# Interleaved rotary embedding: result tiles beside the tiles of x, in place of results written over x

## The chip, the cores and the metric

One core of one Trainium2 chip. The metric is device time in microseconds (us) of one execution. Profiles are of single executions; their span is about 1.8 us shorter than the device time. In the profile's lines DVE is VectorE, ACT is ScalarE, POOL is GpSimd and SP is SyncE; a q after the name (POOLq) is the engine's sequencer, and L56 is line 56 of that run's kernel. A transfer lands when its completion is signalled to the engines that wait for it.

## The reference

```python
# x: (8, 2048, 16, 64) fp32; cos, sin: (2048, 32) fp32
x1, x2 = x[..., 0::2], x[..., 1::2]          # pairs along the head dimension
out1 = x1 * cos - x2 * sin                   # cos, sin per position, the same for all heads
out2 = x1 * sin + x2 * cos
out  = interleave(out1, out2)                # (8, 2048, 16, 64) fp32
```

x and out are 67.1 MB each. There are 8 batches, so one batch is 8.39 MB in fp32, or 4.19 MB once it is cast to bf16.

## The kernel before

A batch is one bf16 tile of 128 partitions x 16 positions x 1024 columns (32 KB per partition). A load reads fp32 from HBM and casts it to bf16 on the way; a store casts back. All big transfers are issued from GpSimd, on one queue. Five tiles hold x, and the rotation is done over x, so the same tile is loaded, rotated, stored, and loaded again. KP is the number of positions in one piece of VectorE's work, NX the number of tiles for x; HEAD and TAIL are the few positions at the start and the end that take another path:

```python
    KP = 4; NX = 5; HEAD = 2; TAIL = 4
    # ... s_tab holds (sin, -sin) pairs, c_tab (cos, cos) pairs, both bf16 ...
    def load(b, k0=0):     # x of batch b from HBM to a tile, cast to bf16
        nc.gpsimd.dma_start(out=tiles[b][:, k0:], in_=x_t[b, :, k0:])
    def store(b, k1=K):
        nc.gpsimd.dma_start(out=out_t[b, :, :k1], in_=tiles[b][:, :k1])
    def rotate(b, k0, k1):
        # ...
        nc.vector.tensor_tensor(out=rows(qt[:, :nk]), in0=rows(xp), in1=tab(s_tab), op=mult)
        nc.vector.tensor_tensor(out=rows(xp), in0=rows(xp), in1=tab(c_tab), op=mult)
        # q_swap: qt with the two members of each pair exchanged
        nc.vector.tensor_tensor(out=x3, in0=x3, in1=q_swap, op=add)

    # first two positions of batch 0, sin and cos come through SyncE and ScalarE; then:
        load(0, HEAD)
        for b in range(1, NX):
            load(b)
        # ... tables ...
        for b in range(B):
            # ... rotate the batch in pieces of KP positions ...
            if b < B - 1:
                store(b)
            if b >= 1 and b - 1 + NX < B:
                load(b - 1 + NX)          # its tile is free when store(b - 1) has landed
        store(B - 1, K - TAIL)
        # the last 4 positions of the last batch: cast by ScalarE (after store B-2 has landed), stored by SyncE
```

## Time and profile before

| what | before |
|---|---|
| device time | 317.53 us, median of 3 runs (317.43 to 317.65) |
| profiled span | 315.8 us |
| VectorE busy | 221.8 us (70%), its last instruction ends at 265.6 us |
| DMA, software queue | 97.0% of the span |
| HBM traffic | 67.63 MB read, 67.11 MB written: 427 GB/s over the span |

The first view is the page's table of 40 slices (each digit is a busy share in tenths) and, below it, its table of queues: packets, megabytes, and the share of the 16 DMA engines' time. The software queue (q0 software_dynamic) holds the transfers that GpSimd issues.

```profile
DVE  0009999999999999999999994799708996000000
...
DMA  9999999999999999999999999999999999999997
...
q0 software_dynamic: 2304, 98.04, 97.0%
```

The Trainium skill, "HBM Reference", section "Specifications (TRN2)", has 358 GB/s per core in its table and, in the text below it, about 425 GB/s for a core that streams alone, bounded by its DMA engines; this kernel runs on one core, and its 427 GB/s, loads and stores together, agree with the second.

VectorE has slack at both ends. The DMA engines have none: 9 in every slice but the last.

The second view is the table of waits of the kernel before: who waited for whom, total us, number of times, longest.

```profile
ACT xt L117 <- DMA out_dram<-xt: 286.8, 1, 286.8
POOL out_dram L59 <- DVE xt L80: 153.9, 5, 50.0
POOL xt L56 <- DMA out_dram<-xt: 95.6, 3, 39.7
...
DVE qt L74 <- DMA xt<-in_x_dram: 16.7, 2, 10.8
```

GpSimd waits 95.6 us for stores before it may issue loads 5, 6 and 7, which is the wait that the change takes away. But a wait of the engine that *issues* transfers is lost time only if the queue runs dry meanwhile.

The third view is GpSimd's part of the order of time: start, duration, engine, line, what was issued, and in brackets the idle time before it.

```profile
121.98 0.53 POOL L56 DMA_DIRECT2D xt<-in_x_dram  x1 [39.72 <-DMA out_dram<-xt]
...
141.30 0.53 POOL L56 DMA_DIRECT2D xt<-in_x_dram  x1 [18.27 <-DMA out_dram<-xt]
...
179.95 0.53 POOL L56 DMA_DIRECT2D xt<-in_x_dram  x1 [37.59 <-DMA out_dram<-xt]
```

The load lines (L56) come out the moment a store has landed, so they date the landings: store 0 at 121.98 us, store 1 at 141.30, and store 2, with load 5 in front of it, at 179.95. One transfer takes 19.3 us and two take 38.65, in order of issue. That is 8.39 MB in 19.3 us: 435 GB/s, counted on the fp32 side. At 54 us GpSimd had issued five loads and a store, six transfers or some 116 us of work, so the queue is full and far behind.

The fourth view gives stretches of the span: VectorE's, ScalarE's and GpSimd's busy time (and instructions), the granted clock, the mean share of the DMA engines, and GB/s on the destination side (a load counts only its bf16 bytes, so pure loads read about half of what pure stores do). The view counts each packet whole in the stretch in which it starts, and one packet of these transfers keeps its DMA engine for about 2.4 us (2.43 us for a load, 2.45 us for a store, in this trace's packet records). So shares can exceed 1.00, shares of stretches of 2 to 3 us swing between about 0.5 and 1.2 while the engines are full, and a row of zeros begins up to 2.4 us before the engines are really empty. Where it matters below, the ends of an empty stretch are read from the packet records in the run's trace, which hold the start and the length of every packet.

```profile
0.00:54.00 54.00, 29.72 (x19) 3.18 (x2) 3.00 (x9) 1.00 0.99 223
54.00:122.00 68.00, 67.01 (x30) 0.00 (x0) 1.10 (x3) 1.00 1.02 285
122.00:180.00 58.00, 57.15 (x26) 0.00 (x0) 2.14 (x5) 1.00 1.01 353
180.00:237.60 57.60, 40.44 (x18) 0.00 (x0) 2.07 (x4) 1.00 1.02 300
237.60:295.60 58.00, 27.51 (x12) 0.00 (x0) 0.53 (x1) 1.00 1.00 429
295.60:316.00 20.40, 0.00 (x0) 3.70 (x2) 0.00 (x0) 1.00 0.88 373
```

The DMA share is full in every stretch up to the last transfer. The packet records say it more sharply: from 5 to 305 us an engine was without a packet for 0.05 us on average.

The last view is two groups of VectorE's instructions, same line at two widths: count, busy us, mean ns.

```profile
L74 DVE TENSOR_TENSOR qt<-xt,s_tab 128x4096 bf16<-128x4096 bf16 x31 | 71.1, 2293 | 17.7 <-DMA xt<-in_x_dram 16.7
...
L74 DVE TENSOR_TENSOR qt<-xt,s_tab 128x2048 bf16<-128x2048 bf16 x2 | 2.4, 1222 | 0.0
```

Doubling the columns from 2048 to 4096 adds 1071 ns, 0.523 ns per column. The Trainium skill, "VectorE: DVE Perf Modes", section "The perf-mode tier table", gives 1224 ns for a bf16 `tensor_tensor` of 2048 columns; the trace agrees (1222 to 1226 ns).

### The profile page before, as it was taken

The numbers are of one execution on the slowest core, as the hardware profiler recorded it, in microseconds if no ns is written. First come the engines' busy times: TensorE is split into PE (matmuls) and PEld (weight loads), VectorE is DVE, ScalarE is ACT, GpSimd is POOL, SyncE is SP. The second block draws the span as 40 slices with busy tenths as digits, with TensorE's granted clock in tenths as the row PEclk, the third lists the DMA queues.
The fourth block names the chain that finished last, engine by engine and source line by source line (L and its number), as shares of the span: only waits on it lengthen the run. The fifth ranks groups of instructions, "written<-read, shape, count | busy, mean of one in ns | idle before, by whom it ended". The sixth has DMA issues, their size and how long they took to land.

```text
span 315.8 us, 198 instructions
## 1 busy us (share of the span) xinstructions
DVE 221.8 (70%) x102; ACT 6.9 (2%) x4; POOL 8.8 (3%) x20
## 2 busy tenths in 40 slices
DVE  0009999999999999999999994799708996000000
ACT  2100000000000000000000000000000000000400
POOL 3000000000000001010000100000000000000000
DMA  9999999999999999999999999999999999999997
GB/s 267 211 248 203 199 208 257 199 199 245 220 199 266 398 465 465 398 332 246 220 398 398 390 208 199 448 481 266 199 266 465 398 398 506 423 398 440 427 427 299
DMA packets 3025, 101.72 MB, mean 322 GB/s; under 512 B 336, under 2 KB 336, under 8 KB 848
## 3 DMA queue, kind: packets, MB, share of 16 engines
q0 software_dynamic: 2304, 98.04, 97.0%
q1 hardware_dynamic: 432, 2.88, 2.4%
q10 hardware_dynamic: 288, 0.79, 0.6%
q14 instruction: 1, 0.01, 0.0%
HBM read 67.63 MB, written 67.11 MB: 427 GB/s over the span
## 4 chain that ended last, share of the span: by engine, by line
another core or an unknown queue 91%; DMA 2%; ACTq 1%; ACT 1%; issue 0%
DMA st<-in_x_dram 2%; ACTq L145 1%; ACT xt L93 1%; ACT L93 0%; ACT xt L117 0%; ACTq L117 0%; ACTq L93 0%
## 5 line engine op out<-in xcount | busy, mean ns | idle before, releaser
L74 DVE TENSOR_TENSOR qt<-xt,s_tab 128x4096 bf16<-128x4096 bf16 (+1 forms) x33 | 73.5, 2228 | 17.7 <-DMA xt<-in_x_dram 16.7
L80 DVE TENSOR_TENSOR xt<-xt,qt 128x4096 bf16<-128x4096 bf16 (+1 forms) x33 | 73.5, 2228 | 1.1
L75 DVE TENSOR_TENSOR xt<-xt,c_tab 128x4096 bf16<-128x4096 bf16 (+1 forms) x33 | 73.5, 2228 | 1.1
L95 DVE CAST s_tab<-sin_sb 128x512 bf16<-128x512 f32 x1 | 0.5, 454 | 23.8 <-DMA sin_sb<-in_sin_dram 23.8
L59 POOL DMA_DIRECT2D out_dram<-xt x8 | 4.3, 533 | 153.9 <-DVE xt L80 153.9
L56 POOL DMA_DIRECT2D xt<-in_x_dram x8 | 4.4, 560 | 96.4 <-DMA out_dram<-xt 95.6
L117 ACT COPY xt<-xt 1x1 bf16<-1x1 bf16 x1 | 0.2, 194 | 286.8 <-DMA out_dram<-xt 286.8
L118 ACT CAST st<-xt 128x4096 f32<-128x4096 bf16 x1 | 3.6, 3598 | 0.0
L93 ACT CAST xt<-st 128x2048 bf16<-128x2048 f32 x1 | 1.9, 1897 | 0.0
L93 ACT ACT_TABLE_LOAD x1 | 1.3, 1283 | 5.7 <-DMA st<-in_x_dram 5.7
L97 DVE CAST c_tab<-cos_sb 128x1024 bf16<-128x1024 f32 x1 | 0.7, 684 | 0.0
L96 DVE TENSOR_SCALAR s_tab<-sin_sb 128x512 bf16<-128x512 f32 x1 | 0.4, 444 | 0.0
L134 POOL MEMSET const-float32-0.0<- 128x1 f32 x1 | 0.1, 99 | 0.2 <-issue 0.2
L134 POOL MEMSET const-bfloat16-1.0<- 128x1 bf16 x1 | 0.1, 102 | 0.0
L134 POOL MEMSET const-float32-1.0<- 128x1 f32 x1 | 0.1, 99 | 0.0
L134 POOL MEMSET const-uint8-127<- 128x1 uint8 x1 | 0.1, 99 | 0.0
## 6 DMA issues: line engine op xcount, KB each, us to landing
xt<-in_x_dram POOLq DMA_DIRECT2D x7, 4096.0 KB, 57.6
out_dram<-xt POOLq DMA_DIRECT2D x1, 6144.0 KB, 53.0
xt<-in_x_dram POOLq DMA_DIRECT2D x1, 3584.0 KB, 22.8
out_dram<-st SPq DMA_DIRECT2D x1, 2048.0 KB, 15.5
st<-in_x_dram ACTq DMA_DIRECT2D x1, 512.0 KB, 5.1
st<-in_x_dram SPq DMA_DIRECT2D x1, 512.0 KB, 4.9
sin_sb<-in_sin_dram ACTq DMA_DIRECT2D x1, 256.0 KB, 22.6
cos_sb<-in_cos_dram SPq DMA_DIRECT2D x1, 256.0 KB, 18.6
```

The lines of the kernel that those rows point to most:

```text
L56: nc.gpsimd.dma_start(out=tiles[b][:, k0:], in_=x_t[b, :, k0:])
L59: nc.gpsimd.dma_start(out=out_t[b, :, :k1], in_=tiles[b][:, :k1])
L74: nc.vector.tensor_tensor(out=rows(qt[:, :nk]), in0=rows(xp), in1=tab(s_tab), op=mult)
L75: nc.vector.tensor_tensor(out=rows(xp), in0=rows(xp), in1=tab(c_tab), op=mult)
L80: nc.vector.tensor_tensor(out=x3, in0=x3, in1=q_swap, op=add)
L93: nc.scalar.copy(out=tiles[0][:, :HEAD], in_=head[:, :HEAD])
L95: nc.vector.tensor_copy(out=s2[:, :, 0], in_=sin_sb)
L96: nc.vector.tensor_scalar_mul(s2[:, :, 1], sin_sb, -1.0)
L97: nc.vector.tensor_copy(out=c_tab.rearrange("p k (i j) -> p (k i) j", j=2), in_=cos_sb.to_broadcast([P, K * D2, 2]),)
L118: nc.scalar.copy(out=tail, in_=tiles[B - 1][:, K - TAIL :])
L134: nc = _bacc.Bacc("TRN2", target_bir_lowering=False, num_devices=1)
L145: with _tile.TileContext(nc) as tc:
```

## The change

The intent: a tile of x is read by VectorE only, the result goes to a tile of its own, so a load waits for VectorE and no longer for a store. The multiply by sin is done over x (x is dead after it), which saves the scratch tile. VectorE's pieces grow from 4 to 8 positions. To find room, x has 3 tiles in place of 5, the results 3, and the staging for the first and last positions and for sin and cos borrows tiles of x.

```diff
-    KP = 4
+    KP = 8
-    NX = 5
+    NX = 3
+    NO = 3
 ...
-        nc.vector.tensor_tensor(out=rows(qt[:, :nk]), in0=rows(xp), in1=tab(s_tab), op=mult)
-        nc.vector.tensor_tensor(out=rows(xp), in0=rows(xp), in1=tab(c_tab), op=mult)
+        nc.vector.tensor_tensor(out=rows(op), in0=rows(xp), in1=tab(c_tab), op=mult)
+        nc.vector.tensor_tensor(out=rows(xp), in0=rows(xp), in1=tab(s_tab), op=mult)
 ...
-        nc.vector.tensor_tensor(out=x3, in0=x3, in1=q_swap, op=add)
+        nc.vector.tensor_tensor(out=o3, in0=o3, in1=x_swap, op=add)
 ...
         load(0, HEAD)
-        for b in range(1, NX):
-            load(b)
+        load(1)
 ... (tables)
+        load(2)            # its tile held sin, cos and the first positions
         for b in range(B):
 ...
-            if b < B - 1:
-                store(b)
-            if b >= 1 and b - 1 + NX < B:
-                load(b - 1 + NX)
-        store(B - 1, K - TAIL)
+            if b + NX < B:
+                load(b + NX)
+            store(b, K if b < B - 1 else K - TAIL)
 ... (the tail as before, from a tile of x's pool)
```

More of the change, by code (lines that the diff above doesn't have):

```diff
@@ L42, with fp32_tile @@
     xpool = ctx.enter_context(tc.tile_pool(name="xpool", bufs=NX))
-    qpool = ctx.enter_context(tc.tile_pool(name="qpool", bufs=1))
-    stage = ctx.enter_context(tc.tile_pool(name="stage", bufs=1))
-    cos_sb = consts.tile([P, K * D2], fp32)
-    sin_sb = consts.tile([P, K * D2], fp32)
+    opool = ctx.enter_context(tc.tile_pool(name="opool", bufs=NO))
     c_tab = consts.tile([P, K, D], bf16)
     s_tab = consts.tile([P, K, D], bf16)
-    tiles = {}
+    xs, os = {}, {}
+    def fp32_tile():
+        return xpool.tile([P, K // 2, HD], fp32, name="xt")
     def load(b, k0=0):
-        if b not in tiles:
-            tiles[b] = xpool.tile([P, K, HD], bf16, name="xt")
-        nc.gpsimd.dma_start(out=tiles[b][:, k0:], in_=x_t[b, :, k0:])
+        if b not in xs:
+            xs[b] = xpool.tile([P, K, HD], bf16, name="xt")
+        nc.gpsimd.dma_start(out=xs[b][:, k0:], in_=x_t[b, :, k0:])
     def store(b, k1=K):
-        nc.gpsimd.dma_start(out=out_t[b, :, :k1], in_=tiles[b][:, :k1])
+        nc.gpsimd.dma_start(out=out_t[b, :, :k1], in_=os[b][:, :k1])
     def rotate(b, k0, k1):
         nk = k1 - k0
-        xp = tiles[b][:, k0:k1]
-        qt = qpool.tile([P, KP, HD], bf16, name="qt")
+        xp = xs[b][:, k0:k1]
+        op = os[b][:, k0:k1]
         def rows(a):
@@ L72, in tab @@
             )
-        nc.vector.tensor_tensor(out=rows(qt[:, :nk]), in0=rows(xp), in1=tab(s_tab), op=mult)
-        nc.vector.tensor_tensor(out=rows(xp), in0=rows(xp), in1=tab(c_tab), op=mult)
-        q_swap = dataclasses.replace(
-            qt, offset=qt.offset + 1, ap=[qt.ap[0], [2, nk * HD // 2], [-1, 2]]
-        )
-        x3 = xp.rearrange("p k (a j) -> p (k a) j", j=2)
-        nc.vector.tensor_tensor(out=x3, in0=x3, in1=q_swap, op=add)
+        nc.vector.tensor_tensor(out=rows(op), in0=rows(xp), in1=tab(c_tab), op=mult)
+        nc.vector.tensor_tensor(out=rows(xp), in0=rows(xp), in1=tab(s_tab), op=mult)
+        x_swap = dataclasses.replace(
+            xp, offset=xp.offset + 1, ap=[xp.ap[0], [2, nk * HD // 2], [-1, 2]]
+        )
+        o3 = op.rearrange("p k (a j) -> p (k a) j", j=2)
+        nc.vector.tensor_tensor(out=o3, in0=o3, in1=x_swap, op=add)
     with tc.manual_schedule():
-        head = stage.tile([P, TAIL, HD], fp32, name="st")
+        pre = fp32_tile()
+        cos_sb = pre[:, HEAD, : K * D2]
+        sin_sb = pre[:, HEAD + 1, : K * D2]
         for k in range(HEAD):
             q = (nc.sync, nc.scalar)[k % 2]
-            q.dma_start(out=head[:, k : k + 1], in_=x_t[0, :, k : k + 1])
+            q.dma_start(out=pre[:, k : k + 1], in_=x_t[0, :, k : k + 1])
         nc.sync.dma_start(out=cos_sb, in_=cos_t)
@@ L89 @@
         load(0, HEAD)
-        for b in range(1, NX):
-            load(b)
-        nc.scalar.copy(out=tiles[0][:, :HEAD], in_=head[:, :HEAD])
+        load(1)
+        nc.scalar.copy(out=xs[0][:, :HEAD], in_=pre[:, :HEAD])
         s2 = s_tab.rearrange("p k (i j) -> p (k i) j", j=2)
@@ L100 @@
         )
+        load(2)
         for b in range(B):
-            if b == 0:
-                rotate(b, 0, HEAD)
-                rotate(b, HEAD, KP)
-            for k0 in range(KP if b == 0 else 0, K, KP):
+            os[b] = opool.tile([P, K, HD], bf16, name="ot")
+            for k0 in range(0, K, KP):
                 rotate(b, k0, k0 + KP)
-            if b < B - 1:
-                store(b)
-            if b >= 1 and b - 1 + NX < B:
-                load(b - 1 + NX)
-        store(B - 1, K - TAIL)
-        tail = stage.tile([P, TAIL, HD], fp32, name="st")
-        nc.scalar.copy(out=tiles[B - 2][:1, 0, :1], in_=tiles[B - 1][:1, K - 1, :1])
-        nc.scalar.copy(out=tail, in_=tiles[B - 1][:, K - TAIL :])
-        nc.sync.dma_start(out=out_t[B - 1, :, K - TAIL :], in_=tail)
+            if b + NX < B:
+                load(b + NX)
+            store(b, K if b < B - 1 else K - TAIL)
+        tail = fp32_tile()
+        nc.scalar.copy(out=os[B - 2][:1, 0, :1], in_=os[B - 1][:1, K - 1, :1])
+        nc.scalar.copy(out=tail[:, :TAIL], in_=os[B - 1][:, K - TAIL :])
+        nc.sync.dma_start(out=out_t[B - 1, :, K - TAIL :], in_=tail[:, :TAIL])
 _INS = ['x', 'cos', 'sin']
```

## The prediction

> **What bounds the kernel now.** The 16 DMA engines, from start to end. The slice row for DMA is 9 in 39 of 40 slices; the queue table gives the software queue 97.0% of the span. VectorE is busy 70% and done at 265.6 of 315.8 us (order of time). The waits give landings on that queue: store 0 at 121.98 us, store 1 at 141.30, store 2 at 179.95 (load 5 ahead of it), load 6 at 199.03, load 7 at 237.67 (with store 3), store 6 at 295.6 (with stores 4, 5). That is 19.3 us per 8.39 MB of fp32, load or store, alternating or in a row, in order of issue: 435 GB/s. The Trainium skill, "DMA: Bandwidth & Descriptors", section "Where 436 GB/s comes from", states 435.2 GB/s for the 16 engines; the trace agrees, counted on the fp32 side. 16 transfers of 19.3 us are 309 us; the start (first bytes, sin, cos) adds about 4 us and the end 1 to 2.
>
> **What the change does.**
> - Removes the waits of loads 5 to 7 for stores 0 to 2 (95.6 us of GpSimd waiting). None of it is on the critical path: the queue held issued work throughout.
> - Halves VectorE's instruction count. 2048 columns take 1.22 us, 4096 take 2.293, so 8192 should take 4.43 us (estimate). Six per batch with the 0.035 us step between: 26.8 us against 27.9. VectorE busy falls from 221.8 to about 214 us, off the path.
> - Adds: load 2 waits for the tables (about 25 us; the staging lies in its buffer); the result tile of batch b waits for store b-3.
> - Bytes moved: unchanged.
>
> **Replaying the queue**, 19.3 us each, in issue order L0 L1 L2 L3 S0 L4 S1 L5 S2 L6 S3 L7 S4 S5 S6 S7:
> L2 is issued at 25, queue busy to 43. VectorE ends batch 0 at about 52 and issues L3, S0 (queue busy to 62). Batch 1 ends 79 (queue busy to 100); batch 2, 106 (139); batch 3, 132 (177); batch 4 waits for store 1, ends 165 (216); batch 5, 204 (255); batch 6, 243 (274); batch 7, 281 (293). The queue never runs dry; the thinnest margins are 10 us after batch 0 and 12 us at the end. VectorE's new idle time (about 40 us in batches 4 to 7) costs nothing. The tail is unchanged: ScalarE waits for store 6 at about 295.5 us, casts in 3.6 us, and the last 2 MB share the engines with store 7.
>
> **Predicted time: 317.4 us, range 315.3 to 320.0.** Faster by over 2%: 0.02. Within 2%: 0.95. Slower by over 2%: 0.03.
>
> **Right if:** DMA row 9 in all slices to the end, software queue near 97%. GpSimd's waits name VectorE alone; VectorE now waits for stores before the c_tab multiply, 6 to 12 us in each of batches 4 to 7. VectorE busy near 214 us, 4430 ns each at 8192 columns, ending near 281 us. ScalarE's tail copy released at about 295.5 us.
> **Wrong if:** a slice of DMA clearly below 9 in mid-span (near 52-62 or 281-293 us), ScalarE's copy released later than 298 us, or pairs of load and store taking other than 38.6 us.
>
> **What would make it wrong.** A queue that runs dry because VectorE starts late (sin lands at 23.8 us now; 10 us later would cost) or takes longer per column at 8192. Strict alternation of loads and stores running at another rate than long runs of one kind (unlikely: both show 19.3 us).

## The result, and the profile after

| what | before | after |
|---|---|---|
| device time, median of 6 runs each | 317.48 us (317.40 to 317.65) | 317.51 us (317.35 to 317.71) |
| profiled span | 315.8 us | 315.7 us |
| VectorE busy | 221.8 us | 212.8 us |
| VectorE's last instruction ends | 265.6 us | 283.5 us |

The ratio is 1.0001, with a 95% interval of 0.9989 to 1.0014. Ratios here are the mean time of one kernel's runs over that of the other's of the same rounds, so not quite the ratio of the medians quoted. Executions over 1.5% slower than the fastest of the same kernel are left out of the means.

The same views, after. The slices and the software queue:

```profile
DVE  0009999999999999619992299913999049990000
...
DMA  9999999999999999999999999999999999999996
...
q0 software_dynamic: 2304, 98.04, 97.0%
```

VectorE's row has changed its shape (gaps of idle time from the middle on, and work until later), the DMA row has not, but for one tenth in its last slice.

The waits after. GpSimd waits for VectorE only; what waits for stores now is VectorE, before its first multiply of a batch (and ScalarE at the tail, as before).

```profile
ACT ot L116 <- DMA out_dram<-ot: 286.6, 1, 286.6
POOL xt L57 <- DVE ot L81: 137.4, 5, 35.1
POOL out_dram L60 <- DVE ot L81: 113.8, 3, 38.2
DVE ot L75 <- DMA out_dram<-ot: 45.7, 4, 12.1
```

GpSimd's order of time after (loads are L57). Load 2 goes out when the tables are built; from then on each load and the store beside it are issued as VectorE ends a batch, here load 3 and store 0:

```profile
25.74 0.53 POOL L57 DMA_DIRECT2D xt<-in_x_dram  x1 [23.29 <-DVE c_tab L100]
52.20 0.53 POOL L57 DMA_DIRECT2D xt<-in_x_dram  x1 [25.93 <-DVE ot L81]
52.72 0.54 POOL L60 DMA_DIRECT2D out_dram<-ot  x1
```

VectorE's order of time after: the four multiplies that waited for a result tile, and the last instruction.

```profile
140.95 4.42 DVE L75 TENSOR_TENSOR ot<-xt,c_tab 128x8192 bf16<-128x8192 bf16 x1 [9.53 <-DMA out_dram<-ot]
...
179.53 4.42 DVE L75 TENSOR_TENSOR ot<-xt,c_tab 128x8192 bf16<-128x8192 bf16 x1 [11.98 <-DMA out_dram<-ot]
...
218.23 4.42 DVE L75 TENSOR_TENSOR ot<-xt,c_tab 128x8192 bf16<-128x8192 bf16 x1 [12.10 <-DMA out_dram<-ot]
...
256.88 4.42 DVE L75 TENSOR_TENSOR ot<-xt,c_tab 128x8192 bf16<-128x8192 bf16 x1 [12.05 <-DMA out_dram<-ot]
...
279.05 4.43 DVE L81 TENSOR_TENSOR ot<-ot,xt 128x8192 bf16<-128x8192 bf16 x1
```

The stores that free these tiles land at about 141, 179.5, 218.2 and 256.9 us, steps of 38.6 to 38.7 us for one load and one store. That is the pace of the kernel before.

Stretches of the span after:

```profile
0.00:54.00 54.00, 29.92 (x10) 3.18 (x2) 2.99 (x9) 1.00 0.99 223
54.00:122.00 68.00, 67.66 (x16) 0.00 (x0) 2.11 (x4) 1.00 1.02 285
122.00:180.00 58.00, 36.29 (x10) 0.00 (x0) 2.11 (x4) 1.00 1.01 353
180.00:237.60 57.60, 45.26 (x11) 0.00 (x0) 0.54 (x1) 1.00 1.02 300
237.60:295.60 58.00, 33.65 (x8) 0.09 (x1) 1.06 (x2) 1.00 1.00 429
295.60:316.00 20.40, 0.00 (x0) 3.67 (x2) 0.00 (x0) 1.00 0.88 373
```

Beside the table before, every DMA share and every GB/s is the same. VectorE's busy time per stretch differs by up to 21 us (57.15 against 36.29 in the third), and the DMA engines do not notice: by the packet records they were again without a packet for under 0.05 us on average between 5 and 305 us.

The group of VectorE's first multiply:

```profile
L75 DVE TENSOR_TENSOR ot<-xt,c_tab 128x8192 bf16<-128x8192 bf16 x16 | 70.7, 4420 | 45.8 <-DMA out_dram<-ot 45.7
```

The estimate of 4430 ns for 8192 columns is met within 10 ns.

### The profile page after: what moved, and what is told of

Same layout as the page of the kernel before. It is cut to its first block, busy times and chain, and to the rows that moved or that the text cites. A ratio compares the mean times of both kernels' runs of the same rounds, so it can differ in the third digit from the quotient of the medians.

```text
span 315.7 us, 146 instructions
## 1 busy us (share of the span) xinstructions
DVE 212.8 (67%) x51; ACT 6.9 (2%) x4; POOL 8.8 (3%) x20
## 4 chain that ended last, share of the span: by engine, by line
another core or an unknown queue 61%; DMA 16%; DVE 9%; ACT 1%; issue 0%; POOL 0%; ACTq 0%
DMA out_dram<-ot 16%; DVE xt L76 3%; DVE ot L81 3%; DVE ot L75 3%; ACT xt L117 1%; DVE c_tab L100 0%; POOL xt L57 0%; ACTq L116 0%; ACT ot L116 0%; ACTq L117 0%
## 5 line engine op out<-in xcount | busy, mean ns | idle before, releaser
L75 DVE TENSOR_TENSOR ot<-xt,c_tab 128x8192 bf16<-128x8192 bf16 x16 | 70.7, 4420 | 45.8 <-DMA out_dram<-ot 45.7
L81 DVE TENSOR_TENSOR ot<-ot,xt 128x8192 bf16<-128x8192 bf16 x16 | 70.8, 4425 | 0.5
L76 DVE TENSOR_TENSOR xt<-xt,s_tab 128x8192 bf16<-128x8192 bf16 x16 | 70.8, 4425 | 0.5
L57 POOL DMA_DIRECT2D xt<-in_x_dram x8 | 4.4, 547 | 161.4 <-DVE ot L81 137.4
L60 POOL DMA_DIRECT2D out_dram<-ot x8 | 4.3, 535 | 113.8 <-DVE ot L81 113.8
L117 ACT CAST xt<-ot 128x4096 f32<-128x4096 bf16 x1 | 3.6, 3604 | 0.0
L96 ACT CAST xt<-xt 128x2048 bf16<-128x2048 f32 x1 | 1.9, 1897 | 0.0
L100 DVE CAST c_tab<-xt 128x1024 bf16<-128x1024 f32 x1 | 0.7, 683 | 0.0
```

Of the source, the lines that this page charges most:

```text
L57: nc.gpsimd.dma_start(out=xs[b][:, k0:], in_=x_t[b, :, k0:])
L60: nc.gpsimd.dma_start(out=out_t[b, :, :k1], in_=os[b][:, :k1])
L75: nc.vector.tensor_tensor(out=rows(op), in0=rows(xp), in1=tab(c_tab), op=mult)
L81: nc.vector.tensor_tensor(out=o3, in0=o3, in1=x_swap, op=add)
L96: nc.scalar.copy(out=xs[0][:, :HEAD], in_=pre[:, :HEAD])
L100: nc.vector.tensor_copy(out=c_tab.rearrange("p k (i j) -> p (k i) j", j=2), in_=cos_sb.to_broadcast([P, K * D2, 2]),)
```

## The experiments

Theory: the 16 DMA engines carry a fixed number of bytes at 19.3 us per 8.39 MB. Whatever waits for whom costs nothing until the queue runs dry, and then it costs what the queue stood empty. Main rival: the old wait and the new one both cost, about the same, and have cancelled. The expectations rest on a replay of the queue: 19.3 us per batch transferred, in order of issue, each issued when VectorE and the tiles allow. Eleven kernels were run. Each had 4 runs, beside 7 of the kernel before.

### 1. All transfers, no rotation

```diff
 ...
-            os[b] = opool.tile([P, K, HD], bf16, name="ot")
-            for k0 in range(0, K, KP):
-                rotate(b, k0, k0 + KP)
+            os[b] = oa if b < B - 1 else ob     # two tiles, zeroed once
 ...
```

> Wrong result on purpose: the rotation is taken out, the stores send two zeroed result tiles, and no load or store waits for VectorE's work on x. All transfers keep their number, size, queue and issue order. Theory (the queue's bytes set the time, 19.3 us per 8.39 MB): within 1% of before, 315 to 318 us. Rival (two waits of equal cost have cancelled, so the chain of load, rotation and store is in the time): the time falls once the chain is gone, by over 2%, to under 311 us.

Measured: 317.75 us against 317.72, ratio 1.0001 (0.9987 to 1.0016). Stretches of this run (columns as above):

```profile
54.00:122.00 68.00, 0.00 (x0) 0.00 (x0) 2.11 (x4) 1.00 1.02 285
122.00:180.00 58.00, 0.00 (x0) 0.00 (x0) 2.65 (x5) 1.00 1.01 353
...
237.60:295.60 58.00, 0.00 (x0) 0.00 (x0) 0.00 (x0) 1.00 1.00 429
```

From 54 us on, with VectorE at rest (its last work is the zeroing of the two tiles) and no load or store waiting for it, the shares and rates are those of both real kernels. Loads still wait here for the earlier load of their tile, but the queue never empties. The main rival falls: there was no hidden cost of waits to cancel.

### 2. The change with VectorE's pieces as before

```diff
-    KP = 8
+    KP = 4
```

> The change with VectorE's pieces of 4096 columns as before, so 27.9 us a batch again in place of 26.5. Theory: VectorE is off the path; same within 0.3%, 317.5 us, VectorE busy near 222 us. Rival (halving VectorE's instructions won about what the new wait for stores lost): 9 to 11 us slower, about 328 us.

Measured: 317.60 us, ratio 0.9997 (0.9982 to 1.0012), VectorE busy 218.9 us (expected near 222). The longer instructions had neither won nor lost anything.

### 3. and 4. The change with a slower VectorE

```diff
         nc.vector.tensor_tensor(out=rows(op), in0=rows(xp), in1=tab(c_tab), op=mult)
+        # 3: for the second half of each batch only; 4: always. Same result.
+        nc.vector.tensor_tensor(out=rows(op), in0=rows(xp), in1=tab(c_tab), op=mult)
```

> The change with one multiply per batch done twice (same result): 4.45 us more of VectorE per batch, 35.6 us in all. Theory, from a replay of the queue: it still never runs dry, so 317.5 us, within 0.5%, and VectorE's idle time before its multiplies shrinks from 45.7 to under 20 us. Rival (VectorE's time counts): up to 353 us; half of it would be 335.

Measured: 317.87 us, ratio 1.0007 (0.9991 to 1.0024), with VectorE busy 248.0 us, 35 more than in the change. Its waits for stores:

```profile
DVE ot L75 <- DMA out_dram<-ot: 14.7, 2, 7.6
```

They shrank from 45.7 to 14.7 us. So VectorE's new idle time really was slack: 35 us of work went in and nothing came out at the end.

> The change with both multiplies by cos of each batch done twice: 8.9 us more per batch, 71 us in all. Theory, from the replay: batch 0 still makes its deadline by about 2 us, the queue runs dry once, before the last store, for 15 to 16 us: 333 us (329 to 336), and the profile shows a slice or two of low DMA near 293 to 309 us and none earlier. Rival (VectorE's time counts in full): 388 us; rival (VectorE never counts): 317.5 us.

Measured: 332.73 us against 317.72, ratio 1.0474 (1.0459 to 1.0490): 15.0 us more, for 70 us more VectorE work (283.2 us busy). Stretches near the end (columns as above):

```profile
290.00:298.00 8.00, 7.96 (x3) 0.00 (x0) 0.00 (x0) 1.00 0.64 270
298.00:309.00 11.00, 10.64 (x3) 0.26 (x2) 0.00 (x0) 1.00 0.00 0
```

The last store is issued at 309.0 us, when VectorE ends batch 7. By the packet records the engines run out of work at 296 to 297 us (one at 298.8) and start again at 310.1: they are empty for 13.8 us on average, and this is nearly all of the loss. The expectation said there would be no earlier gap; the trace has a small one, 0.7 us on average near 62 us, as load 3 is issued only at 61.0 us (see the next run). It does not show in the sum because here the last gap takes it up: VectorE works from batch 0 to the end without a pause, and the time is its end plus what is left to store.

### 5. A slower VectorE in batch 0 alone

```diff
+        for _ in range(2 if b == 0 else 0):
+            nc.vector.tensor_tensor(out=rows(op), in0=rows(xp), in1=tab(c_tab), op=mult)
```

> The change with 17.8 us more of VectorE in batch 0 alone (its two multiplies by cos done three times each). VectorE ends batch 0 at about 70 us; the queue has work to about 62 us. Theory, from the replay: dry once, for about 8 us before load 3, and that gap goes to the end whole: 326 us (323 to 328). Rival (VectorE has some 50 us of idle time later in the kernel, so it catches up): 317.5 us. Rival (VectorE counts in full): 335 us.

Measured: 328.12 us against 317.71, ratio 1.0329 (1.0314 to 1.0345): 10.4 us more where the replay said about 8. GpSimd's issue of load 3, the stretches around it, and, from the list of issues, load 2 (issued at 25.62 us) with its KB and the us from issue to landing:

```profile
69.92 0.53 POOL L57 DMA_DIRECT2D xt<-in_x_dram  x1 [43.77 <-DVE ot L83]
```

```profile
60.00:70.00 10.00, 9.93 (x4) 0.00 (x0) 0.08 (x1) 1.00 0.00 0
70.00:71.00 1.00, 1.00 (x1) 0.00 (x0) 0.98 (x2) 1.00 0.00 0
71.00:72.00 1.00, 1.00 (x1) 0.00 (x0) 0.00 (x0) 1.00 2.81 492
...
xt<-in_x_dram POOLq DMA_DIRECT2D x1, 4096.0 KB, 36.9
```

The stretches read zero from 60 us, but that is when the last packets start. Load 2, the last transfer in the queue, lands at 62.5 us (25.62 and 36.9), and its last packets end between 61.6 and 62.3: the replay's 62 was right. At the other end no packet starts when load 3 is issued, at 69.9 us; the first one starts at 71.2, 1.2 us later. So the engines are empty for 9.6 us on average, and nearly all of the 10.4 us is this gap. VectorE has 38.4 us of idle time later in this run, and none of it gives the lost 10 us back: it catches up, the queue cannot. What the replay had left out is the time from the issue to the first packet, which counts when the queue is empty: 1.1 us for the stores and 1.25 us for the loads that end the gaps of runs 4 to 7 and 9. The Trainium skill, "DMA: Bandwidth & Descriptors", section "Anatomy of one DMA — SWDGE (gpsimd) path", puts most of a fixed 2 us of each DMA into the receipt of its last write; these traces show the larger part before the first packet, and only 0.3 to 0.5 us between the end of the last packet and the landing (here 62.27 to 62.55 us). For the change itself it means that batch 0's margin is about 61.9 - 52.2 - 1.2 = 8.5 us (estimate), not the 10 predicted.

### 6. and 7. Fewer tiles in the change

```diff
-    NO = 3
+    NO = 2            # 6: x 3, results 2
```
```diff
-    NX = 3
-    NO = 3
+    NX = 2
+    NO = 2            # 7: x 2, results 2; load 1 is now issued after the tables
```

> The change with 2 result tiles in place of 3. Now batch b waits for store b-2. Theory, from the replay: store 6 and store 7 come to a dry queue, 8 to 9 and 7 us: 333 us (329 to 337), all of the loss in the second half. Rival (tiles of results beyond one do not matter as the load waits for VectorE anyway): 317.5 us.

Measured: 334.47 us against 317.71, ratio 1.0529 (1.0513 to 1.0545), 16.8 us more. Two stretches of the second half:

```profile
274.00:284.00 10.00, 9.93 (x4) 0.00 (x0) 0.04 (x1) 1.00 0.00 0
...
305.00:310.00 5.00, 4.97 (x2) 0.00 (x0) 0.00 (x0) 1.00 0.00 0
```

The two dry stretches are where the replay had them, before stores 6 and 7 (issued at 283.96 and 310.46 us). By the packet records the engines are empty for 9.6 us (from about 275.5 to 285.1) and 7.2 us (304.4 to 311.6), together the whole 16.8; the replay had 8 to 9 and 7, without the 1.1 us from issue to first packet.

> The change with 2 tiles of x and 2 of results, 4 in all; load 1 then waits for the tables. Theory, from the replay: dry for about 3 us before load 1, 7 before load 2 and 9 before the last store: 336 us (331 to 341). To be read beside the kernel before with 4 tiles of x in all, from which the replay expects no loss.

Measured: 339.15 us, ratio 1.0679 (1.0661 to 1.0696), 21.4 us more where the replay had 18.5 (336 against 317.5). By the packet records the engines are empty for 4.1 us (about 23.3 to 27.4), 6.5 us (47.4 to 53.9) and 9.6 us (306.8 to 316.3), before loads 1 and 2 and the last store, where the replay had 3, 7 and 9; that is 20.1 of the 21.4 us, and the rest was not traced.

### 8. and 9. Fewer tiles in the kernel before

```diff
-    NX = 5
+    NX = 4            # 8
```
```diff
-    NX = 5
+    NX = 3            # 9
```

> The kernel before with 4 tiles in place of 5: each load waits for the store of its tile, one batch sooner. Theory, from the replay: the queue never runs dry, 317.5 us within 0.5%, though GpSimd's waits for stores grow. Rival (a load that waits for a store costs time, which is what the change set out to remove): slower by over 2%, above 324 us.

Measured: 317.79 us against 317.71, ratio 1.0004 (0.9989 to 1.0019). The wait of loads for stores in this run:

```profile
POOL xt L56 <- DMA out_dram<-xt: 85.8, 4, 29.6
```

Four loads now wait for stores in place of three, the time is the same. In sum these waits did not grow, as expected, but fell from 95.6 to 85.8 us, while GpSimd's waits for VectorE before stores grew from 153.9 to 183.3 us. So this is the change's target made more frequent, not longer, and it costs nothing. Four tiles in place, with a scratch tile and the staging (156 KB per partition without the tables), do what the change does with six (192 KB): its layout with 3 and 2 tiles took 334.47 us, and with four in all 339.15 us (runs 6 and 7).

> The kernel before with 3 tiles in place of 5. Theory, from the replay: the queue runs dry at the last store for about 10 us and for under 1 us once earlier: 328 us (323 to 332). Here the wait of loads for stores at last costs time. Rival (only the depth of 2 matters): 317.5 us.

Measured: 322.28 us against 317.65, ratio 1.0147 (1.0132 to 1.0162): 4.6 us more, less than half of the 10 expected. The end of this run in order of time (GpSimd's last store, VectorE's last add), and the stretch before that store:

```profile
298.53 0.53 POOL L59 DMA_DIRECT2D out_dram<-xt  x1 [31.13 <-DVE xt L80]
...
302.93 2.29 DVE L80 TENSOR_TENSOR xt<-xt,qt 128x4096 bf16<-128x4096 bf16 x1
```

```profile
294.00:299.00 5.00, 4.93 (x3) 0.00 (x0) 0.47 (x1) 1.00 0.01 0
```

By the packet records the engines are empty for 4.1 us on average before the last store (from about 295.6 to 299.7) and for 0.8 us near 82 us, together about the loss of 4.6. The replay had that store wait for all of batch 7. But it carries 12 of 16 positions, and with pieces of 4 it goes out when three of four pieces are done, about 7 us before VectorE's end. A term of the replay was wrong, not its principle. (The change, with pieces of 8, must wait for both; in its normal form the queue covers that.) At nearly the same memory, 124 KB here and 128 KB in run 7, in place took 322.28 us and the new layout 339.15; the two also differ in the pieces and in when load 1 is issued.

### 10. and 11. What the 19.3 us are made of

Both kernels move 8 loads and 8 stores without a cast, between HBM and fp32 tiles. Their outputs are wrong, which doesn't matter for the times. In run 10 SyncE issues the loads and ScalarE the stores, in run 11 GpSimd issues all.

```diff
 ...
-            xs[b] = xpool.tile([P, K, HD], bf16, name="xt")
-        nc.gpsimd.dma_start(out=xs[b][:, k0:], in_=x_t[b, :, k0:])
+            xt = xpool.tile([P, K, HD], fp32, name="xt")
+            nc.sync.dma_start(out=xt, in_=x_t[b])      # 11: nc.gpsimd
 ...
+            nc.scalar.dma_start(out=out_t[b], in_=ot)  # 11: nc.gpsimd; ot zeroed once
```

> Wrong result on purpose: 8 loads of 8.39 MB to fp32 tiles and 8 stores from a zeroed fp32 tile, without a cast, issued from SyncE and ScalarE; no tables, no rotation. The SBUF side moves twice the bytes of the real kernels, the HBM side the same. Theory (the rate is set by the 4-byte side, 435 GB/s, whatever the cast and the queue): 311 to 317 us. Rival (the cast or the software queue holds the engines back): faster by over 2%, under 311 us.

Measured: 322.67 us, ratio 1.0170 (1.0153 to 1.0187). Outside of the range that the theory gave, on the slow side. The rival, that the cast or the software queue holds the engines back, would have made it faster, and falls for the queue; for the cast it falls only if the doubled bytes on the SBUF side cost nothing by themselves, which no run separates. The run moves 432 GB/s from 80 to 300 us and ends with single packets that arrive until about 317 us.

> Wrong result on purpose: as the fp32 run before, but all its 16 transfers issued from GpSimd, on the one queue of the real kernels. That run was 5 us slower than before, with its last packets trickling in over the final 7 us. If the two interleaved queues let some engines fall behind: the trickle goes, 314 to 318 us. If it is the fp32 tiles on the SBUF side (or engines that are unequal by themselves): it stays at 321 to 324 us.

Measured: 321.80 us, ratio 1.0139 (1.0122 to 1.0156). So it is not the two queues. The Trainium skill, "DMA: Bandwidth & Descriptors", section "Issuing engines are not separate DMA queues", says that DMAs run on the same 16 DMA engines whichever engine issues them; that agrees, as two queues (322.67 us) were no faster than one (321.80 us). GpSimd's issues here date the landings of loads, two transfers apart (each load waits for the earlier load of its tile):

```profile
83.58 0.53 POOL L53 DMA_DIRECT2D xt<-in_x_dram  x1 [38.22 <-DMA xt<-in_x_dram]
...
200.82 0.53 POOL L53 DMA_DIRECT2D xt<-in_x_dram  x1 [37.80 <-DMA xt<-in_x_dram]
```

From 83.58 to 200.82 us, six transfers take 19.54 us each, against 19.3 with a cast. 16 times 0.24 us would be 3.8 us, most of the loss of 4.2 (this run moves 0.5 MB less, as it needs no sin and cos). But the six may not stand for all: from 240 to 300 us this run moves 435 GB/s, the full rate. So twice the bytes on the SBUF side go along with about 1% more time: halving them by the cast wins next to nothing. Where and why the last 1% is lost is not settled.

## Why the prediction was right

The number alone was no feat: it is the time before. What the prediction risked was the replay, and most of its times can be checked.

- **The bound.** Right. DMA row full and software queue at 97.0% in both; run 1 shows the same time without any rotation.
- **The removed wait is off the critical path.** Right. The 95.6 us vanished from GpSimd and the time stayed; run 8, with four such waits in place of three, stayed too.
- **VectorE.** 212.8 us busy (predicted about 214), 4420 to 4425 ns per instruction (4430), ending at 283.5 us (281); it waits for stores 9.5 to 12.1 us in each of batches 4 to 7 (6 to 12). The end is 2.5 us late because batch 4's wait ended at 140.95 us, where the replay had about 138 (165 less the batch's 26.8). Run 2 shows that the shorter busy time was worth nothing.
- **The new wait costs nothing.** Right: run 3 filled 35 us more work in and lost nothing.
- **The replay.** The queue never ran dry, as said, and ScalarE's tail copy was released at 295.51 us (295.5). The margins were overstated: about 8.5 us after batch 0 and not 10 (run 5), about 10 at the end and not 12 (store 7 is issued at 283.8 us, its packets need 1.1 us more, and store 6 lands at 295.5). The term left out is the 1.1 to 1.25 us from issue to first packet. In the prediction it did not matter; in runs 4 to 7 it is about 1 us of each gap.
- **Pairs of load and store take 38.6 us** in the new order also: VectorE's waits end 38.6 to 38.7 us apart. Strict alternation runs at the old rate.

Why no version faster than both was tried: transfers alone in this form take 317.75 us. 16 times 19.3 is 309 us, sin and cos are 0.5 MB or 1.2 us at the same rate, and what remains is the start and the last landing. A rearrangement of waits or of VectorE's work alone does not change these; that is argued, not tried. Which part of the chip sets the 435 GB/s stays open.

## What to carry to other kernels

Before removing a wait, ask whether the resource that bounds the kernel stood still during it: an issuing engine that waits while its queue holds work loses nothing, and the wait will only move elsewhere. Replay the queue with the measured time per transfer, add the time from issue to first packet where the queue is empty (1.1 to 1.25 us here), and look for the moment when it would run dry; the smallest margin tells how much slower the other engines may become, and a gap, once there, is not made up later. Where the margin is ample, spend the memory elsewhere: four tiles in place were as fast here as six in the new layout.

## What the Trainium skill lacked or had wrong

- "DMA: Bandwidth & Descriptors", section "Where 436 GB/s comes from", gives 435.2 GB/s for 16 ports on the SBUF side and says that the ports are the bottleneck. It doesn't say which side counts when a DMA casts. Here casting transfers move 8.39 MB in 19.3 us counted on the fp32 (HBM) side, 435 GB/s, while the SBUF side carries half of that, about 217 GB/s; without a cast the same time holds within about 1% (19.54 us). The number agrees, but a limit of the ports alone would leave casting transfers room to be faster, and they were not.
- The same page has no statement of what a cast in a DMA costs. Here a transfer with a cast took 19.3 us and one without, of the same bytes in HBM, 19.54 us (run 11); as the latter moves twice the bytes on the SBUF side, the cost of the cast alone is not shown.
- "DMA: Bandwidth & Descriptors", section "Anatomy of one DMA — SWDGE (gpsimd) path", puts most of the 2 us of a DMA into the receipt of its last write. In runs 4 to 7 and 9, where transfers from GpSimd meet an empty queue, the first packet starts 1.1 to 1.25 us after the start of the issue, and the landing follows the end of the last packet by 0.3 to 0.5 us. (Whether the record of a packet itself contains a receipt, the traces do not tell.)
